# Plain float32 output and query projections, early low parts on VectorE, and six held PSUM banks in layer 1's expert matrix product

## The chip, the cores and the metric

The kernel runs on one core of one Trainium2 chip. The metric is the device time of one execution in microseconds: the median of 3 runs is 4076.9 us (4074.23 to 4081.48). The engines are named as the profile names them: PE (TensorE's matrix multiply; PEld is its weight load), DVE (VectorE), ACT (ScalarE), POOL (GpSimd), SP (the engine that issues most loads). Each runs its own instructions strictly in the order in which they stand in its queue; a semaphore wait at the head holds back all that is behind it.

## The reference

Two layers over 512 latent tokens and 256 context tokens of width 1024. Layer 0 mixes tokens with a state-space model, layer 1 with latent attention. Each is followed by an output projection, a residual and a layer norm, and by a PEER channel mixer with 16,384 experts:

```python
h = layer_norm(ALPHA * h + mod[2] * (y @ w_o))              # after the mixer
t = h * (1 + mod[4]) + mod[3]
q = (t @ w_q).reshape(n_tok, 8, 2, 64)                      # queries, 8 heads
s = einsum('thsd,hsnd->thsn', q, keys); sv, si = top_k(s, 16)
# top 16 of the 16 x 16 sums per head -> 128 experts idx and gates per token
act = gelu(einsum('td,tkd->tk', t, u_tab[idx])) * gate
f = einsum('tk,tkd->td', act, v_tab[idx])
h = layer_norm(ALPHA * h + mod[5] * f)
```

All is float32, and the choice of experts (top_k) hangs on small differences of the scores.

## The kernel before

Tokens stand in six tiles of 128: tiles 0 and 1 are the context, 2 to 5 the latents. In layer 0 the PEER mixer treats tiles 2 to 5 as *dense* and 0, 1 as *gathered*; in layer 1 tiles 4, 2, 3 are dense, 5 is gathered, and the context needs no output. A gathered tile fetches its 256 rows of `peer_u` and `peer_v` per token position by indirect DMAs on POOL's queue (`gather`, L1275), and DVE multiplies each (L1282, L1287). Dense tiles are multiplied with all experts: a block is 128 experts, `dense_u` (L1137) forms Gelu(U·H) for one block and all dense tiles, DVE multiplies it with the gates, and L1207 multiplies the result `A` with the block's rows of V. The gates come from `gate_matrix`: one-hot matrices `e` and `o` on DVE and ACT, products `g_ps` on PE (L1102), written to memory as `gm` and read back as `Gt`.

TensorE reads float32 in two ways here. A plain float32 matmul stands twice in the trace. An F32R matmul runs once, at lower precision; to keep the precision the kernel splits both operands into a high and a low part and adds three products (high·high, high·low, low·high). `split` (L302 to L306) makes the parts: ACT casts the high part (L305), and DVE or POOL, as the caller says, subtracts it (L306).

Order of the work: `merge` interleaves Python generators by clocks that the program keeps (the numbers that the generators yield), `pipeline(steps, n)` issues the preparation of a step n steps ahead of its work, and the tile framework then places the instructions on each engine. After the mixer of a layer, `out_steps` (output projection of a pair of tiles, 16 steps of 128 input rows by 512 output columns, then the norms) and `query_steps` (transpose, then 8 heads of the query projection) of the pairs run beside `route` (the top-16 searches, almost all DVE) of the tiles whose queries are ready, and beside `ahead`, which does the U products of some blocks early and stores them in memory (`ged`): blocks 0 to 39 in layer 0 and 0 to 47 in layer 1. Then come the gate matrices with the rest of these early blocks, and then `dense` beside `gather`. `dense` accumulates 8 blocks in PSUM for one half of the 1024 columns at a time and then adds the banks into `oacc` in SBUF (L1213, L1215); the U products of 8 blocks stand between; the last half group is done tile by tile (L1228). All PSUM tiles share 8 banks of 128x512 float32. SBUF tiles come from shared rings (`t4`: 20 of 4 KB, `t2`: 8 of 2 KB, `row`: 5 of 4 KB), so a load waits until an earlier tile of its place is no longer read.

Stages of the profiled execution, by their landmarks: to 374 us the state-space layer; 374 to 675 output and query projections of layer 0 with the routing of the context; 675 to 1130 routing of the latents, early blocks and gate matrices; 1130 to 2354 `dense` of layer 0; 2354 to 2668 attention; 2668 to 2790 projections of layer 1; 2790 to 3155 routing, early blocks and gate matrices; 3155 to 4040 `dense` of layer 1; then the last norms.

Of the kernel before, what the change touches and what calls it, by code (L numbers as in the profile page):

```python
# [41 lines left out]
NPOOL = 0  # L42
FA = 1.0
R0, R1 = 2.25, 3.0
A0, A1 = 40, 48
GA = 3
TL, PW, XM = 3, 2, 2.0
FG0, FG1 = 50.0, 5.0
# [59 lines left out]
class Net:  # L108
# [662 lines left out]
    def out_steps(self, l, pair, src, parts, first, rows):  # L771


        nc = self.nc
        st = {}

        def begin(_):
            st["y"] = parts()
            return 0.0

        def prep(hf, k):
            if (hf, k) == (1, 0):
                st["h"] = []
                for ti in pair:
                    h = self.t4([128, D], "h")
                    self.load(h, first(ti))
                    st["h"].append(h)
            w = self.t2([128, 512], "wo")
            self.load(w, src[k * 128:(k + 1) * 128, hf * 512:(hf + 1) * 512])
            W = self.t4([128, 2, 512], "Wos", F32R)  # L790
            self.split(W[:, 0], W[:, 1], w, nc.gpsimd if k % 4 else nc.vector)
            return W

        def work(hf, k, W):
            if k == 0:
                st["op"] = [self.ps([128, 512], "op") for _ in pair]
            for i, op in enumerate(st["op"]):
                for n, (x, y) in enumerate(((0, 0), (0, 1), (1, 0))):
                    nc.tensor.matmul(out=op, lhsT=st["y"][k // 2][:, x, k % 2, i * 128:(i + 1) * 128], rhs=W[:, y],
                                     start=(k == 0 and n == 0), stop=(k == KD - 1 and n == 2))  # L800
# [17 lines left out]
        return ([(lambda: None, begin)]  # L818
                + [(lambda hf=hf, k=k: prep(hf, k), lambda W, hf=hf, k=k: work(hf, k, W)) for hf in range(2) for k in range(KD)]
                + [(lambda: None, norm)])  # L820

    def s5_layer(self, dense, gather):
# [23 lines left out]
                    self.row_bc(a["ln_b"], 0, "lnb", tile=tile)]  # L846

        def out(pair):
            s = 1 if pair[0] < 2 else 0
            per = (2, 4)[s]  # L850
            r0 = pair[0] * 128 - (256, 0)[s]

            def parts():
                ys = []
                for x in range(4):
                    ys.append(self.t4([128, 2, 2, 256], "ys", F32R))
                    y = self.yT[s][2 * x // per][:, 2 * x % per:2 * x % per + 2, r0:r0 + 256]
                    self.split(ys[-1][:, 0], ys[-1][:, 1], y, nc.gpsimd)
                return ys

            return self.out_steps(0, pair, a["s5_w_o"], parts,
                                  lambda ti: a["ctx"][0, ti * 128:(ti + 1) * 128, :] if ti < 2
                                  else a["x"][0, (ti - 2) * 128:(ti - 1) * 128, :], lambda: self.rows2)

# [9 lines left out]
        def memory_ctx(_):  # L874
            self.rows2 = rows(1, self.big)
            return 0.0

        Hc = self.t16([128, 2, KD, 256], "Hc", F32R)
        self.h1 = {}
        (m0, q0), (m1, q1), (m2, q2) = (self.query_steps(0, (0, 1), lambda: Hc),  # L880
                                        self.query_steps(0, (2, 3), lambda: self.Hall[:, :, :, 0:256]),
                                        self.query_steps(0, (4, 5), lambda: self.Hall[:, :, :, 256:512]))
# [25 lines left out]
    def query_steps(self, l, pair, H):  # L908
# [5 lines left out]
        st = {}  # L914

        def modulate(i, ti):
            mT = self.mod_transpose(self.h1[pair][i], l, s, 3)
            c = slice(i * 128, (i + 1) * 128)
            H_ = H()
            self.split(H_[:, 0, :, c], H_[:, 1, :, c], mT, nc.vector)  # L920
            if ti not in self.tiles:
                m = self.m[ti] = self.t4([128, D], "m")
                for k4 in range(2):
                    tp = self.ps([128, 4, 128], "m_ps")
                    for k in range(4):
                        PE.transpose(out=tp[:, k, :], in_=mT[:, k4 * 4 + k, :], identity=self.ident)
                    S.copy(out=m[:, k4 * 512:(k4 + 1) * 512], in_=tp)
            return 1.0

        def prep(h):  # L930
            w = self.row([128, KD, 128], "wq")
            self.load(w, self.a["peer_w_q"][l, h])
            W = [self.t4([128, KD, 128], f"wq{x}", F32R) for x in range(2)]
            self.split(W[0], W[1], w, nc.gpsimd)
            return W

        def work(h, W):
            if h == 0:
                st["q"] = [self.t4([128, 8, 128], "qT") for _ in pair]
            if h % 2 == 0:  # L940
                st["p"] = self.ps([128, 2, 256], "qp")
            n = 0
            for k in range(KD):
                for x, y in ((0, 0), (0, 1), (1, 0)):
                    PE.matmul(out=st["p"][:, h % 2], lhsT=W[x][:, k, :], rhs=H()[:, y, k, :], start=(n == 0),
                              stop=(n == 3 * KD - 1))
                    n += 1
# [357 lines left out]
    def peer_out(self, l, ti, f, rows=None):  # L1305
# [5 lines left out]
        V.tensor_tensor(out=f, in0=f, in1=m5, op=ALU.mult)  # L1311
# [18 lines left out]

    def dense_out(self, l, ti):
        f = self.oacc[self.tiles.index(ti)]
        self.dump(f"f{l}_{ti}", f)
        return self.peer_out(l, ti, f, self.rows)


    def mla(self, dense, gather):
# [179 lines left out]
        order = gather + dense  # L1517

        def out(pair):
            q0 = (min(pair) - 2) * 128  # L1520

            def parts():
                os = []
                for o in oT:
                    os.append(self.t4([128, 2, 2, 256], "os", F32R))
                    for i, ti in enumerate(pair):
                        c = slice(i * 128, i * 128 + 128)
                        self.split(os[-1][:, 0, :, c], os[-1][:, 1, :, c], o[:, :, (ti - 2) * 128:(ti - 1) * 128], V)
                return os

            return self.out_steps(1, pair, a["mla_w_o"], parts, lambda ti: self.hd[ti], lambda: r)
# [8 lines left out]
        self.aheads = self.ahead(1, A1, 4)  # L1540
# [82 lines left out]
```

## Time and profile before

| | |
|---|---|
| median of 3 runs | 4076.9 us (4074.23 to 4081.48) |
| profiled execution | 4075.69 us; its span, first to last instruction, 4073.6 us |
| PE busy | 3664.2 us, 90% of the span |
| PEld busy | 3029.0 us, 74% |
| DVE busy | 3231.9 us, 79% |
| ACT busy | 1558.1 us, 38% |
| POOL busy | 1638.1 us, 40% |
| granted PE clock, mean | 0.953 of full speed |

Busy times are unions over an engine's instructions. A matmul's row is longer than the distance to the next, since matmuls overlap; what a matmul costs in a row of many is the distance between two starts. "Idle before" is the time in which the engine stood still just ahead of the instructions of a group, with what ended it.

### The profile page before, as it was taken

To read this page: it belongs to the slowest core of one execution; us is meant where nothing else is said; L and a number is where in the kernel's file an instruction comes from. 1 tells how busy PE (TensorE), PEld (TensorE's weight loads), DVE (VectorE), ACT (ScalarE), POOL (GpSimd) and SP (SyncE) were. 2 spreads that over 40 slices of the span, in tenths; PEclk is the share of its full clock that TensorE was granted. 3 is DMA by queue.
4 is the path that set the end of the run, shared out by engine and by line. 5 is a ranking of instruction groups with operands and counts; after the bars stand their busy time and mean duration, and the time that the engine had idled before them with its cause. 6 is when DMAs were issued, how large, how long until landed. Compare 5 with 4: busy or idle time off the path is not lost.

```text
span 4073.6 us, 54069 instructions
## 1 busy us (share of the span) xinstructions
PE 3664.2 (90%) x18795; PEld 3029.0 (74%) x18795; DVE 3231.9 (79%) x6315; ACT 1558.1 (38%) x2804; POOL 1638.1 (40%) x1140
## 2 busy tenths in 40 slices
PE   5759879789789999999999989989888899999998
PEld 3527868678667888778888855568888678999997
DVE  8784498988877788988888844469987678888887
ACT  1321335357632322233332233354467333433333
POOL 4744346245412455556555300055344113334341
PEclk6879989899999999999999999999899999999999
DMA  5457234268988899999999820044377888887885
GB/s 178 136 175 249 86 122 156 90 220 272 326 302 293 300 341 342 332 352 340 338 336 342 324 103 3 30 160 149 126 232 256 316 277 321 295 336 283 335 294 215
DMA packets 398450, 986.15 MB, mean 242 GB/s; under 512 B 67040, under 2 KB 147424, under 8 KB 393568
## 3 DMA queue, kind: packets, MB, share of 16 engines
q1 hardware_dynamic: 217120, 501.34, 35.3%
q0 software_dynamic: 110592, 402.70, 28.0%
q10 hardware_dynamic: 70464, 78.65, 5.6%
q8 instruction: 148, 2.42, 0.2%
q14 instruction: 126, 1.03, 0.1%
HBM read 892.28 MB, written 90.21 MB: 241 GB/s over the span
## 4 chain that ended last, share of the span: by engine, by line
PE 45%; issue 10%; DVE 10%; DMA 5%; POOL 5%; ACT 3%; ACTq 0%; POOLq 0%; DVEq 0%; SPq 0%
PE s_ps L1137 20%; PE acc L1207 15%; POOL row L1275 4%; PE g_ps L1102 3%; DMA row<-in_peer_v,idx 2%; DMA W<-in_peer_v 1%; DVE row L1282 1%; PE op_mla L1507 1%; DMA ge<-ged 1%; DVE e L1080 1%; DVE Ws L306 1%; PE acc L1228 1%; DVE f L1287 1%; PE kvp L1365 1%; ACT o L1085 1%
## 5 line engine op out<-in xcount | busy, mean ns | idle before, releaser
L1207 PE MATMUL acc<-Ws,A 128*128 128x512 f32 x5208 | 1202.9, 392 | 63.6 <-ACT A L305 36.3
L1137 PE MATMUL s_ps<-Hs,Uh 128*128 128x512 f32 (+1 forms) x4096 | 1184.8, 371 | 11.2 <-ACT Uh L305 11.2
L1207 PEld LDWEIGHTS acc<-Ws,A 128*128 128x128 f32 x5208 | 981.8, 189 | 280.4 <-ACT A L305 37.0
L1137 PEld LDWEIGHTS s_ps<-Hs,Uh 128*128 128x128 f32 x4096 | 761.5, 190 | 104.9 <-ACT Uh L305 12.6
L1275 POOL DMA_INDIRECT row<-in_peer_u,idx x384 | 513.2, 1336 | 783.2 <-DVE row L1282 712.3
L1137 PE MATMUL s_ps<-Hs,Ul 128*128 128x512 f32 (+1 forms) x2048 | 756.9, 370 | 15.5 <-POOL Ul L306 15.5
L1275 POOL DMA_INDIRECT row<-in_peer_v,idx x384 | 485.6, 1264 | 549.0 <-DVE f L1287 484.8
L1282 DVE SCALAR_TENSOR_TENSOR row<-row,m 128x1024 f32<-128x1024 f32 x384 | 490.4, 1293 | 54.7 <-DMA row<-in_peer_u,idx 53.8
L1287 DVE SCALAR_TENSOR_TENSOR f<-row,act,f 128x1024 f32<-128x1024 f32 x381 | 487.3, 1279 | 39.4 <-DMA row<-in_peer_v,idx 38.4
L305 ACT CAST Ws<-W 128x512 fp32r<-128x512 f32 x512 | 305.5, 619 | 489.0 <-DMA W<-in_peer_v 439.5
L1137 PEld LDWEIGHTS s_ps<-Hs,Ul 128*128 128x128 f32 x2048 | 389.0, 190 | 66.2 <-POOL Ul L306 19.8
L306 DVE TENSOR_TENSOR Ws<-W,Ws 128x512 fp32r<-128x512 f32 x512 | 345.1, 684 | 101.6 <-ACT Ws L305 101.0
L305 ACT CAST Uh<-U 128x1024 fp32r<-128x1024 f32 x256 | 268.1, 1048 | 313.6 <-DMA U<-in_peer_uT 242.6
L306 POOL TENSOR_TENSOR Ul<-U,Uh 128x1024 fp32r<-128x1024 f32 x88 | 227.3, 2585 | 312.3 <-ACT Uh L305 199.0
L1140 ACT ACTIVATE ge<-s_ps 128x512 f32<-128x512 f32 (+1 forms) x256 | 139.1, 544 | 520.4 <-PE s_ps L1137 504.9
L1102 PE MATMUL g_ps<-o,o 128*128 128x128 f32 x1792 | 232.7, 289 | 87.2 <-DVE o L1088 51.7
L1102 PEld LDWEIGHTS g_ps<-o,o 128*128 128x128 f32 x1792 | 223.7, 202 | 96.9 <-ACT o L1085 95.1
L306 POOL TENSOR_TENSOR Wos<-wo,Wos 128x512 fp32r<-128x512 f32 x60 | 87.0, 1476 | 469.9 <-PE tp_ps L286 350.9
L305 ACT CAST A<-ge 128x512 fp32r<-128x512 f32 (+1 forms) x256 | 144.5, 565 | 280.7 <-DVE ge L1188 266.6
L306 DVE TENSOR_TENSOR Ul<-U,Uh 128x1024 fp32r<-128x1024 f32 x168 | 204.9, 1221 | 47.9 <-ACT Uh L305 47.5
L1188 DVE TENSOR_TENSOR ge<-ge,Gt 128x512 f32<-128x512 f32 (+1 forms) x256 | 155.7, 619 | 74.8 <-ACT ge L1140 51.1
L306 DVE TENSOR_TENSOR A<-ge,A 128x512 fp32r<-128x512 f32 (+1 forms) x256 | 158.4, 620 | 45.6 <-ACT A L305 44.7
(346 smaller groups left out, 4631.7 us busy)
## 6 DMA issues: line engine op xcount, KB each, us to landing
U<-in_peer_uT SPq DMA_DIRECT2D x256, 512.0 KB
W<-in_peer_v SPq DMA_DIRECT2D x512, 256.0 KB
gm<-stage ACTq DMA_DIRECT2D x28, 2048.0 KB
ada_wt<-in_ada_w SPq DMA_DIRECT2D x96, 512.0 KB
Gt<-gm SPq DMA_DIRECT2D x16, 2048.0 KB
Gt<-gm SPq DMA_DIRECT2D x16, 1536.0 KB
wq<-in_peer_w_q SPq DMA_DIRECT2D x40, 512.0 KB
wo<-in_s_w_o SPq DMA_DIRECT2D x48, 256.0 KB
```

Of the source, the lines that this page charges most:

```text
L305: self.nc.scalar.copy(out=hi, in_=x)
L306: lo_eng.tensor_tensor(out=lo, in0=x, in1=hi.bitcast(F32), op=ALU.subtract)
L1080: V.tensor_tensor(out=e.rearrange("p s t (i x) -> p (s t) i x", x=2), in0=self.iota128.rearrange("p (i x) -> p i x", x=2).unsqueeze(1).to_ ...
L1085: S.copy(out=o2, in_=e[:, 0])
L1102: PE.matmul(out=gp[:, t, :], lhsT=o[1][:, t4 * 4 + t, :], rhs=o[0][:, t4 * 4 + t, :], start=True, stop=True)
L1137: PE.matmul(out=sp, lhsT=x[:, k, :], rhs=self.Hs[:, y, k, :], start=(n == 0), stop=(n == 3 * KD - 1))
L1140: S.activation(out=ge, in_=sp, func=AF.Gelu)
L1188: V.tensor_tensor(out=gv, in0=gv, in1=Gt[b // SB][:, :, :, b % SB, :], op=ALU.mult)
L1207: PE.matmul(out=acc[hf][d], lhsT=A[b][:, x, c], rhs=Ws[:, y], start=(j == 0 and n == 0), stop=(j == SB - 1 and n == 2))
L1275: GP.indirect_dma_start(out=r, out_offset=None, in_=tab, in_offset=bass.IndirectOffsetOnAxis(ap=ik[:, k:k + 1], axis=0), element_offset=l ...
L1282: x = V.scalar_tensor_tensor(out=r, in0=r, scalar=1.0, in1=m, op0=ALU.mult, op1=ALU.mult, accum_out=act[:, k:k + 1])
L1287: x = V.scalar_tensor_tensor(out=f, in0=r, scalar=act[:, k:k + 1], in1=f, op0=ALU.mult, op1=ALU.add)
```

## The change

Four edits. (1) `out_steps` takes the weights `wo` and the activations as they are: one plain float32 product per step and tile instead of three F32R products, and no split of either operand. (2) `query_steps` does the same with `wq` and the transposed tile; the split of the activations stays where the dense tiles need it for `dense_u`. (3) `ahead` lets DVE instead of POOL make the low part of U, and takes a list of blocks; in layer 1 these are the first 3 of each 8 blocks (48 as before). (4) Layer 1 uses a new `dense_held`: six PSUM banks (three tiles by two halves) collect all 128 blocks, U and V products alternate block by block, the V rows are loaded and split 1024 wide, and the last KL = 2 blocks are multiplied tile by tile; `peer_out` then reads the banks. Layer 0 keeps `dense`.

```diff
-A0, A1 = 40, 48
+A0, A1 = 40, 3
+KU, LH, KL, GQ = 2, 4, 2, 4
 # out_steps
             w = self.t2([128, 512], "wo")
             self.load(w, src[k * 128:(k + 1) * 128, hf * 512:(hf + 1) * 512])
-            W = self.t4([128, 2, 512], "Wos", F32R)
-            self.split(W[:, 0], W[:, 1], w, nc.gpsimd if k % 4 else nc.vector)
-            return W
+            return w
...
-                for n, (x, y) in enumerate(((0, 0), (0, 1), (1, 0))):
-                    nc.tensor.matmul(out=op, lhsT=st["y"][k // 2][:, x, k % 2, i * 128:(i + 1) * 128], rhs=W[:, y], ...)
+                nc.tensor.matmul(out=op, lhsT=y(i, k), rhs=W, start=(k == 0), stop=(k == KD - 1))
 # query_steps
-            W = [self.t4([128, KD, 128], f"wq{x}", F32R) for x in range(2)]
-            self.split(W[0], W[1], w, nc.gpsimd)
-            return W
+            return w
...
-                for x, y in ((0, 0), (0, 1), (1, 0)):
-                    PE.matmul(out=st["p"][:, h % 2], lhsT=W[x][:, k, :], rhs=H()[:, y, k, :], ...)
+            for i in range(2):
+                for k in range(KD):
+                    PE.matmul(out=st["p"][:, h % 2, i * 128:(i + 1) * 128], lhsT=W[:, k, :], rhs=st[i][:, k, :], ...)
 # ahead
-        yield from pipeline([(lambda b=b: self.dense_u_prep(l, b, self.nc.gpsimd), lambda Us, b=b: work(b, Us))
-                             for b in range(n)], LA)
+        yield from pipeline([(lambda b=b: self.dense_u_prep(l, b, self.nc.vector), lambda Us, i=i: work(i, Us))
+                             for i, b in enumerate(blocks)], LA)
+    def dense_held(self, l):
...
+        def products(b, d, Ws):
+            c = slice(d * 128, (d + 1) * 128)
+            for n, (x, y) in enumerate(((0, 0), (0, 1), (1, 0))):
+                for hf in range(2):
+                    PE.matmul(out=acc[d][hf], lhsT=A[b][:, x, c], rhs=Ws[y][:, hf * 512:(hf + 1) * 512],
+                              start=(b == 0 and n == 0), stop=(b == NB - 1 and n == 2))
...
+        steps = us[:KU]
+        for b in range(NB):
+            steps += us[b + KU:b + KU + 1] + [vs[b]]
+        steps += [(lambda: None, lambda _, d=d: finish(d)) for d in range(NT)]
+        yield from pipeline(steps, LH)
 # peer_out
+            for hf in range(2):
+                c = slice(hf * 512, (hf + 1) * 512)
+                V.tensor_tensor(out=f[:, c], in0=acc[hf], in1=m5[:, c], op=ALU.mult)
 # peer
-        merge(self.dense(l), self.gathering)
+        merge(self.dense_held(l) if len(self.tiles) < 4 else self.dense(l), self.gathering)
```

Three places in the queues. First, DVE in layer 0 while it routes a context tile (the rows with `rw` are top-16 searches); the low part of the output weights stands among them:

```order
L976 MAX_INDEX rw_4008<-rw_4008,tk_tmp 128x8
L975 MAX rw_4008<-tk_tmp 128x8
L306 TENSOR_TENSOR Wos<-wo,Wos 128x512
L976 MAX_INDEX rw_4008<-rw_4008,tk_tmp 128x8
L972 MAX rw_4008<-scr 128x8
```

and the same engine there now, where only the evictions `res` of the finished products are left among the searches:

```order
L950 MAX_INDEX rw_3987<-rw_3987,tk_tmp 128x8
L948 MATCH_REPLACE tk_tmp<-rw_3987,cand 128x80
L797 TENSOR_TENSOR res<-op,m_3937 128x512
L949 MAX rw_3987<-tk_tmp 128x8
L797 TENSOR_TENSOR res<-op,m_3937 128x512
```

The split of the weights is gone from the searches. Second, POOL before, at the end of layer 0's queries, where the low parts of the early blocks follow the indirect loads of the gather:

```order
L306 TENSOR_TENSOR wq_5358<-wq,wq_5357 128x1024
L1275 DMA row<-in_peer_u,idx 128x1024
L306 TENSOR_TENSOR Ul<-U,Uh 128x1024 x22
L1275 DMA row<-in_peer_u,idx 128x1024
L306 TENSOR_TENSOR Ul<-U,Uh 128x1024
```

and DVE now, in the routing of the first latent tile, where they stand between the searches:

```order
L946 MAX rw_4789<-cand 128x8
L949 MAX rw_4789<-tk_tmp 128x8
L947 MAX_INDEX rw_4789<-rw_4789,cand 128x8
L306 TENSOR_TENSOR Ul<-U,Uh 128x1024
L950 MAX_INDEX rw_4789<-rw_4789,tk_tmp 128x8
```

POOL keeps indirect loads alone. Third, PE at the start of layer 1's expert product before, where the V products of all 48 early blocks follow in one run:

```order
L1137 MATMUL s_ps<-Hs,Uh 128x384 x2
L1137 MATMUL s_ps<-Hs,Ul 128x384
L1207 MATMUL acc_25631<-Ws,A 128x512 x3
L1207 MATMUL acc_25632<-Ws,A 128x512 x3
L1207 MATMUL acc_25633<-Ws,A 128x512 x3
```

and now, where the last tile's products of the first block are followed by a block of U products:

```order
L1180 MATMUL acc_24481<-Wh,A 128x512
L1180 MATMUL acc_24482<-Wh,A 128x512
L1180 MATMUL acc_24481<-Wl,A 128x512
L1180 MATMUL acc_24482<-Wl,A 128x512
L1180 MATMUL acc_24481<-Wh,A 128x512
L1180 MATMUL acc_24482<-Wh,A 128x512
L1111 MATMUL s_ps<-Hs,Uh 128x384 x2
```

PE now alternates between two banks of one tile, and V and U blocks alternate.

## Rows read from the trace of the kernel before

**Rows 1.** Windows: us, each engine's busy us, then PE clock, DMA share, GB/s.

```profile
374.00:675.00 301.00, 250.76 (x1756) 226.18 (x1755) 196.65 (x699) 117.21 (x208) 131.31 (x76) 0.93 0.41 137
675.00:1130.00 455.00, 371.40 (x2137) 319.20 (x2136) 396.77 (x1026) 252.83 (x442) 199.87 (x105) 0.93 0.67 226
...
2668.00:2790.00 122.00, 108.72 (x671) 94.19 (x670) 91.21 (x243) 68.38 (x131) 78.59 (x41) 0.97 0.48 155
2790.00:3155.00 365.00, 311.88 (x1957) 301.43 (x1957) 317.40 (x892) 212.72 (x365) 164.79 (x79) 0.93 0.60 195
3155.00:4040.00 885.00, 861.00 (x4217) 767.13 (x4216) 709.51 (x1023) 324.19 (x551) 282.91 (x225) 0.99 0.84 305
4040.00:4074.00 34.00, 15.26 (x68) 12.30 (x66) 23.92 (x45) 4.22 (x6) 0.00 (x0) 0.76 0.18 71
```

**Rows 2.** Groups of lines: PE from 535.5 to 680, DVE from 490 to 590.

```profile
L799 PE MATMUL op<-Wos,ys 128*128 128x512 f32 x192 | 52.9, 434 | 28.3 <-DVE Wos L306 26.0 <-POOL Wos L306 1.2 <-ACT Wos L305 1.1
...
L306 DVE TENSOR_TENSOR Wos<-wo,Wos 128x512 fp32r<-128x512 f32 x5 | 4.5, 898 | 0.0
```

**Rows 3.** Timeline pieces: start, us, what, count; F32R and plain float32 matmuls.

```profile
2672.70 34.66 PE L799 MATMUL op<-Wos,os 128*128 128x512 f32 x151
...
673.51 6.69 PE L945 MATMUL qp<-Hs,wq 128*128 128x256 f32 x55
...
497.76 28.41 PE L762 MATMUL zp<-yl,wg 128*128 128x128 f32 x253
...
2491.79 0.19 PEld L1507 LDWEIGHTS op_mla<-pT,v 128*128 128x128 f32 x1 [0.24 <-issue]
...
2495.65 0.19 PEld L1507 LDWEIGHTS op_mla<-pT,v 128*128 128x128 f32 x1 [0.24 <-issue]
```

**Rows 4.** Timeline of POOL and DVE around 2800 us, and of DVE at 524 us.

```profile
2799.60 2.40 POOL L306 TENSOR_TENSOR Ul<-U,Uh 128x1024 fp32r<-128x1024 f32 x1 [0.80 <-ACT Uh L305]
...
2799.64 4.58 DVE L1041 TENSOR_TENSOR oh<-iota,ab 128x2048 bf16<-128x2048 bf16 x2
...
524.59 1.22 DVE L1041 TENSOR_TENSOR oh<-iota,ab 128x2048 bf16<-128x2048 bf16 x1
```

**Rows 5.** Groups of lines on DVE while latents are routed, layer 0, 657 to 850.

```profile
L1041 DVE TENSOR_TENSOR oh<-iota,ab 128x2048 bf16<-128x2048 bf16 x8 | 13.9, 1764 | 0.0
...
L1036 DVE TENSOR_TENSOR ab<-rw 128x128 bf16<-128x128 f32 x4 | 3.2, 798 | 0.1
```

**Rows 6.** The same in layer 1, 2764 to 2960.

```profile
L1041 DVE TENSOR_TENSOR oh<-iota,ab 128x2048 bf16<-128x2048 bf16 x6 | 13.7, 2308 | 0.0
```

**Rows 7.** Groups on DVE among the gate matrices: 850 to 1130, then 2960 to 3155.

```profile
L1282 DVE SCALAR_TENSOR_TENSOR row<-row,m 128x1024 f32<-128x1024 f32 x62 | 94.8, 1540 | 13.2 <-DMA row<-in_peer_u,idx 13.2
...
L1080 DVE TENSOR_TENSOR e<-iota,iT 128x2048 bf16<-128x2048 bf16 x39 | 60.9, 1561 | 26.1 <-ACT iT L1070 25.0 <-PE s_ps L1137 1.2
```

**Rows 8.** Costliest groups of the page: the low part of U on either engine.

```profile
L306 POOL TENSOR_TENSOR Ul<-U,Uh 128x1024 fp32r<-128x1024 f32 x88 | 227.3, 2585 | 312.3 <-ACT Uh L305 199.0 <-issue 47.1 <-DVE rw L975 28.7
...
L306 DVE TENSOR_TENSOR Ul<-U,Uh 128x1024 fp32r<-128x1024 f32 x168 | 204.9, 1221 | 47.9 <-ACT Uh L305 47.5
```

**Rows 9.** Waits (us, times, longest): 675 to 1130, then 2790 to 3155.

```profile
POOL Ul L306 <- ACT Uh L305: 78.2, 19, 15.1
...
POOL Ul L306 <- ACT Uh L305: 117.3, 32, 10.8
```

**Rows 10.** Layer 1's expert product: waits from 3150 to 3420, PE group from 3150.

```profile
PE acc L1207 <- ACT A L305: 14.3, 1, 14.3
...
L1207 PE MATMUL acc<-Ws,A 128*128 128x512 f32 x2232 | 514.3, 391 | 24.0 <-ACT A L305 14.3 <-DVE Ws L306 6.9 <-ACT Ws L305 2.8
```

**Rows 11.** Timeline of the end: PE, then the first and last of DVE.

```profile
4038.78 16.48 PE L1228 MATMUL acc<-Ws,A 128*128 128x512 f32 x72
...
4044.42 0.69 DVE L1231 TENSOR_TENSOR oacc<-acc,oacc 128x512 f32<-128x512 f32 x1 [2.95 <-PE acc L1228]
...
4068.80 1.22 DVE L268 TENSOR_TENSOR h<-h,lnb 128x1024 f32<-128x1024 f32 x1
```

More of the change, by code (lines that the diff above doesn't have):

```diff
@@ L55 @@
 AT = 2
-E0, E1, E2 = 0, 11, 5
-YB, YC = 1, 17
+E0, E1, E2 = 0, 10, 5
 NF, MV = 2, (11, 13, 15)
@@ L769, in glu, with out_steps @@
             nc.vector.tensor_tensor(out=y, in0=y, in1=sg[:, x * per:(x + 1) * per, :], op=ALU.mult)
-    def out_steps(self, l, pair, src, parts, first, rows):
+    def out_steps(self, l, pair, src, y, first, rows):
         nc = self.nc
         st = {}
-        def begin(_):
-            st["y"] = parts()
-            return 0.0
         def prep(hf, k):
@@ L816, in norm @@
             return 0.0
-        return ([(lambda: None, begin)]
-                + [(lambda hf=hf, k=k: prep(hf, k), lambda W, hf=hf, k=k: work(hf, k, W)) for hf in range(2) for k in range(KD)]
+        return ([(lambda hf=hf, k=k: prep(hf, k), lambda W, hf=hf, k=k: work(hf, k, W)) for hf in range(2) for k in range(KD)]
                 + [(lambda: None, norm)])
@@ L848, in out @@
         def out(pair):
[L849 to L861, printed above, removed]
+            return self.out_steps(0, pair, a["s5_w_o"], lambda i, k: self.y_tile(pair[i], k),
                                   lambda ti: a["ctx"][0, ti * 128:(ti + 1) * 128, :] if ti < 2
@@ L916, in modulate @@
         def modulate(i, ti):
[L917 to L921, printed above, removed]
+            mT = st[i] = self.mod_transpose(self.h1[pair][i], l, s, 3)
+            if ti in self.tiles:
+                c = slice(i * 128, (i + 1) * 128)
+                H_ = H()
+                self.split(H_[:, 0, :, c], H_[:, 1, :, c], mT, nc.vector)
+            else:
                 m = self.m[ti] = self.t4([128, D], "m")
@@ L1155, in ahead, with prep_g, prep_u, work_u @@
             yield 1.0
-        yield from pipeline([(lambda b=b: self.dense_u_prep(l, b, self.nc.gpsimd), lambda Us, b=b: work(b, Us))
-                             for b in range(n)], LA)
+        yield from pipeline([(lambda b=b: self.dense_u_prep(l, b, self.nc.vector), lambda Us, i=i: work(i, Us))
+                             for i, b in enumerate(blocks)], LA)
+    def dense_held(self, l):
+        nc, a = self.nc, self.a
+        V, S, PE = nc.vector, nc.scalar, nc.tensor
+        NT = len(self.tiles)
+        TD = NT * 128
+        NB, SB = 128, 8
+        Gt, A, last = {}, {}, {}
+        acc = self.acc = []
+        def prep_g(sb):
+            Gt[sb] = self.t16([128, NT, 4, 8, 32], "Gt")
+            self.load(Gt[sb], self.gm[sb])
+        def prep_u(b):
+            if b == 0:
+                prep_g(0)
+            if b % SB == GQ and b // SB + 1 < NB // SB:
+                prep_g(b // SB + 1)
+            if b in self.early:
+                ge = self.t2([128, TD], "ge")
+                self.load(ge, self.ged[self.early[b]])
+                return ge
+            return self.dense_u_prep(l, b, V)
+        def work_u(b, x):
+            ge = x if b in self.early else self.dense_u(x)
+            gv = ge.rearrange("p (d g t) -> p d g t", d=NT, g=4)
+            V.tensor_tensor(out=gv, in0=gv, in1=Gt[b // SB][:, :, :, b % SB, :], op=ALU.mult)
+            A[b] = self.t4([128, 2, TD], "A", F32R)
+            self.split(A[b][:, 0], A[b][:, 1], ge, V)
+            return 0.0 if b in self.early else 5.2 * NT / 4
+        def prep_v(b):
+            W = self.spare([128, D], "W")
+            self.load(W, a["peer_v"][l * NEXP + b * 128:l * NEXP + (b + 1) * 128, :])
+            Wh, Wl = self.t4([128, D], "Wh", F32R), self.t4([128, D], "Wl", F32R)
+            self.split(Wh, Wl, W, V)
+            return Wh, Wl
+        def products(b, d, Ws):
[4 more added lines that the diff above has]
+                              start=(b == 0 and n == 0), stop=(b == NB - 1 and n == 2))
+        def work_v(b, Ws):
+            if b == 0:
+                acc.extend([self.ps([128, 512], f"acc{d}") for hf in range(2)] for d in range(NT))
+            if b >= NB - KL:
+                last[b] = Ws
+                return 0.0
+            for d in range(NT):
+                products(b, d, Ws)
+            return 5.2 * NT / 4
+        def finish(d):
+            for b in last:
+                products(b, d, last[b])
+            return 1.3 * KL
+        yield from self.aheads
+        us = [(lambda b=b: prep_u(b), lambda x, b=b: work_u(b, x)) for b in range(NB)]
+        vs = [(lambda b=b: prep_v(b), lambda x, b=b: work_v(b, x)) for b in range(NB)]
+        steps = us[:KU]
[3 more added lines that the diff above has]
+        yield from pipeline(steps, LH)
@@ L1331, in dense_out @@
     def dense_out(self, l, ti):
-        f = self.oacc[self.tiles.index(ti)]
-        self.dump(f"f{l}_{ti}", f)
+        f = (self.acc if len(self.tiles) < 4 else self.oacc)[self.tiles.index(ti)]
         return self.peer_out(l, ti, f, self.rows)
@@ L1519, in out @@
         def out(pair):
[L1520 to L1531, printed above, removed]
+            return self.out_steps(1, pair, a["mla_w_o"],
+                                  lambda i, k: oT[k // 2][:, k % 2, (pair[i] - 2) * 128:(pair[i] - 1) * 128],
+                                  lambda ti: self.hd[ti], lambda: r)
         p, q = tuple(order[:2]), tuple(order[2:])
@@ L1539, in mla @@
         self.gathering = self.gather(1, R1)
-        self.aheads = self.ahead(1, A1, 4)
+        self.aheads = self.ahead(1, [b for b in range(128) if b % 8 < A1], 4)
         self.gates = self.gate_matrices(4)
```

33 lines of the change are left out of this document (16 added, 17 removed).

## The prediction

> **What bounds the kernel now.** I read the windows by stage first, then PE's groups and its idle time in the two stages of projections, the pitch of each kind of matmul in the timeline, DVE's and POOL's groups where the low parts move, and last the waits and the end. The reader is to see three kinds of stage in [rows 1]. In layer 1's expert product (3155 to 4040) PE is busy 861.0 of 885 us: there only PE's idle time can be won. In the routing and gate stages DVE is the fullest engine (396.8 of 455 us and 317.4 of 365), so what is added to DVE there is paid and what is taken off is won. In the projections neither is full: PE is busy 250.8 of 301 us in layer 0, and stands 28.3 us ahead of the output products, 26.0 of it waiting for five low parts of weights, `Wos`, that DVE makes in 0.898 us each but only when they get through its row of searches [rows 2].
>
> The sum is made against the profiled execution, 4075.69 us; the median is 1.2 us above it, which I add at the end.
>
> **A. Plain products, layer 0.** F32R matmuls of 512 columns start 0.2285 us apart: (34.66 − 0.39)/150, the last one's own time taken off; of 256 columns 0.1187: (6.69 − 0.28)/54. A plain one of 128 columns stands twice, (28.41 − 0.275)/252 = 0.1117 a record, and of 512 columns (2495.65 − 2491.79)/9 = 0.429 a record [rows 3]. The last two come from other lines with the same shapes. A pair's output goes from 96 × 0.2285 = 21.9 to 64 × 0.429 = 27.5 us (+5.5), its queries from 192 × 0.1187 = 22.8 to 256 × 0.1117 = 28.6 (+5.8). Three pairs of layer 0 add 34 us to PE. The last queries (5.8) lie beside routing, where DVE is the bound. PE has 301 − 250.8 = 50.2 us idle in this stage; apart from the 28.3 of `Wos` that is 22, and I let half of it, 11, take up work: 34 − 5.8 − 11 = +17. Against it, the `Wos` idle goes (−28.3), and with it the slowness of the products behind each pause: 192 of them were busy 52.9 us [rows 2] where their pitch gives 43.9 (−9; the granted clock in the stage is 0.93 [rows 1]). A = 17 − 28.3 − 9 = −20. Next late there is DVE with the context's routing; it loses the five `Wos` and the context's splits, and its searches wait for queries, which come sooner. Bounds: −37 if all idle takes up work, 0 if DVE sets the end (a rival below).
>
> **B. Low parts on DVE, routing of the latents, layer 0.** On POOL a low part took 2.585 us, 88 times; on DVE 1.221, 168 times [rows 8]. So 88 × 1.221 = 107 us come to DVE, in the stages where it is the bound. What comes back stands in [rows 4]: while POOL's `Ul` ran, the same `oh` took 2.29 us a piece, and 1.22 without it. In the 193 us of [rows 5], `oh` lost 8 × (1.764 − 1.22) = 4.4 and `ab` 4 × (0.798 − 0.28) = 2.1 us; over about nine such groups of two-input operations I come to 25. About 23 low parts fall into that stretch: 28 to be paid. B = +3 (bounds −25 if they only fill idle, +28 if nothing comes back).
>
> The Trainium skill, "SBUF — State Buffer", section "Who interferes with whom", says that VectorE and GpSimd share one port pair under an exclusive lock, and that nothing else between them contends; 2.29 against 1.22 us in [rows 4] agrees. By that rule the give-back ends where POOL has no arithmetic left, so the indirect loads that POOL keeps would take nothing from DVE; no row here shows it.
>
> **C. Gate matrices.** Between 850 and 1130 the gather's products lost 62 × (1.540 − 1.22) = 19.8 us, with `e` and `o` about 32; 17 low parts cost 20.7. Between 2960 and 3155 `e` lost 39 × (1.561 − 1.22) = 13.3, with the other groups about 32; 21 low parts cost 25.6 [rows 7]. So DVE's load falls by 12 and 7 us. DVE is not full here (it waits 13.2 us for rows and 26.1 for ACT), so I put −5 on the path; bounds −19 and 0.
>
> **D. Projections of layer 1.** Products before: 2 × 21.9 + 2 × 22.8 = 89.5 us by pitch in a window of 122, with 95 other matmuls; so some 20 us are idle or off pitch (13.3 are idle [rows 1]). The change adds 2 × 5.5 + 5.8 up to the first routing, 16.8, and takes away the splits of weights and activations ahead of the products. These about cancel: D = −1, bounds −4 and +17.
>
> **E. Routing, layer 1.** In [rows 6] `oh` lost 6 × (2.308 − 1.22) = 6.5, all groups about 22; 27 low parts cost 33. +11, of which DVE's idle time there takes a little: E = +8, bounds −12 and +33.
>
> **F. Held banks.** PE's work is the same: 128 blocks × 18 products (2232 and 72 before [rows 10, 11]) and 80 blocks of U. From 3155 to PE's last end, 4038.78 + 16.48 = 4055.3, are 900.3 us with 861.0 + 15.3 busy: 24.0 idle. 14.3 of this is one wait for the first `A` [rows 10], which needs the first gates from memory and stays. The other 10 come from weights whose splits on DVE or ACT are late; with U and V blocks alternating, DVE's need per block is even, and 96 additions into `oacc` of 0.69 us [rows 11] go, 66 us of a DVE that is busy 709.5 of 885 us. F = −10, bounds −24 (all idle goes) and +16 (a rival below).
>
> **G. The end.** DVE works through three tiles from 4044.42 to 4070.02, 8.5 us each, and the span ends 18.3 us after PE [rows 11]. Now a tile's last two blocks are 12 products, 2.7 us, so the first tile is ready 5.5 us before PE's end T. Without the addition into `oacc` I take 8 us a tile: DVE is done at T − 5.5 + 24 = T + 18.5, and with the 3.6 us from DVE's last to the span's end (4073.6 − 4070.0) the span ends at T + 22. G = +4, bounds 0 and +8.
>
> Sum: −20 + 3 − 5 − 1 + 8 − 10 + 4 = −21, that is 4055 in the profiled execution and 4056 at the median.
>
> **Rivals.**
>
> *R1, slower: DVE inherits POOL's wait.* A `Ul` needs `Uh`, ACT's cast, and ACT's queue has Gelu ahead of it, which needs PE. POOL stood 78.2 and 117.3 us for it [rows 9] with only the gather behind it; now searches and one-hot matrices stand behind it. If DVE takes over a quarter of these 195.5 us, 49, the sum is −21 + 49 = +28: 4105. It decides from a mean stall of (21 + 8)/88 = 0.33 us per `Ul`. For it: DVE itself waited 47.5 us for `Uh` over its 168 [rows 8], 0.28 each. Against: POOL's waits are those of an engine that had nothing else to do, while DVE has 193/23 = 8 us of other work between two low parts, in which `Uh` is cast.
>
> *R2, no change: PE's idle in A was not the bound.* If DVE's searches of the context set when latent routing starts, A is 0, the rest −1: 4076. For it: DVE is at 197 of 301 us and nearly full late in the stage. Against: its searches wait for PE's queries, too.
>
> *R3, more: the port pays twice.* If C is wholly on the path (−19 in place of −5) and E is taken up by idle (0 in place of +8): −21 − 14 − 8 = −43, 4033. For it: the gather behind POOL's low parts runs sooner, too, and ends C's 13.2 us wait for rows. Against: ACT and PE set part of those stages.
>
> *R4, the held banks don't do what they should.* Six of eight banks are held, and two remain for U products and their Gelu. If each of the 80 U blocks makes PE wait 0.2 us for a bank, F is +16 in place of −10: +5, 4082. For it: PE starts the next block only when ACT has read the bank before. Against: a V block of 18 products, 4.1 us, stands between two U blocks.
>
> *R5, slower: DVE pays its low parts in full.* If the losses in [rows 5, 6] come from something other than POOL's `Ul`, B is +28 and E +33: −21 + 25 + 25 = +29, 4106. For it: both stages have DVE as the fullest engine. Against: [rows 4] has the same instruction at both durations within one routing pattern. The Trainium skill, "Perfetto Trace Analysis", section "Optimizing Scalar/DVE Operations", points this way: it advises moving work off a saturated VectorE, and doubts only that a move between engines that share a port helps.
>
> **How the numbers follow.** What a measurement of this kernel can tell from no change is about 0.2%, 8 us. Forecast 0.45 (of it 0.44 faster, 0.01 same), R3 0.22, R2 0.12 (0.10 same, 0.01 on each side), R4 0.08 (half same, half slower), R1 0.11, R5 0.02. Faster: 0.44 + 0.22 + 0.01 = 0.67; same: 0.01 + 0.10 + 0.04 = 0.15; slower: 0.01 + 0.04 + 0.11 + 0.02 = 0.18. The range reaches from 4022 (R3 with F near its lower bound) to 4090 (R4 with E at 16); the forecast's own is 4038 to 4070, from A between −28 and −10 and E between 0 and 16.
>
> **What would show it.** Right: no `Wos` and no idle of PE on DVE ahead of `op`, though its records are 0.43 apart; queries at 0.112 a record; `oh` at a mean near 1.22; latent routing starting some 20 us sooner; PE's idle in layer 1's expert product near 14 us at its start; PE's end to the end of the span about 22. Wrong: DVE standing ahead of `Ul` for over 0.3 us each, mainly for ACT's `Uh` (R1); PE standing for a bank at `s_ps` (R4); plain 512-column records longer than 0.43 us, each 0.05 of which costs five pairs 16 us; DVE without idle before latent routing, with PE done long before (R2).

## The result and the profile after

The changed kernel takes 4108.2 us (median of 4 runs, 4104.54 to 4108.89) against 4076.4 for the kernel before: a ratio of 1.0068, 95% interval 1.0048 to 1.0088 (the medians alone give 1.0078). It is slower by some 30 us where 20 us faster was forecast, and above the range's upper end of 4090. Its profiled execution has a span of 4105.9 us against 4073.6.

To see where these 32.3 us went I cut both spans at the same landmarks: the end of the last query product of layer 0, of the last `rw` of its searches, of its last `g_ps`, and so on. The last four columns belong to experiments below (plain products alone, low parts on GpSimd, low parts a step later, and the best version). All numbers are us of one profiled execution each.

| stage | before | after | plain | GpSimd | later | best |
|---|---|---|---|---|---|---|
| to the last query product, layer 0 | 680.3 | 666.5 | 664.5 | 664.7 | 662.7 | 664.6 |
| searches of the latents | 151.5 | 150.6 | 143.5 | 143.7 | 153.0 | 148.1 |
| gate matrices, layer 0 | 264.3 | **291.7** | 265.2 | 265.2 | 259.2 | 257.0 |
| expert product 0, attention, projections 1 | 1692.0 | 1697.2 | 1696.4 | 1693.4 | 1689.8 | 1690.1 |
| searches, layer 1 | 172.4 | 175.5 | 169.4 | 169.2 | 170.6 | 162.0 |
| gate matrices, layer 1 | 192.1 | **201.0** | 191.3 | 191.2 | 179.6 | 178.9 |
| expert product 1, to PE's end | 902.7 | 904.5 | 904.7 | 906.1 | 902.1 | 903.0 |
| from PE's end to the span's end | 18.3 | 18.9 | 18.3 | 19.0 | 19.0 | 19.2 |

The loss is in the gate matrices: +27.4 and +8.9. Windows of these two stages in the changed kernel (columns as in [rows 1]):

```profile
818.00:1109.00 291.00, 229.88 (x1421) 204.14 (x1420) 218.30 (x265) 191.26 (x350) 82.81 (x54) 0.94 0.77 252
...
2981.00:3183.00 202.00, 165.03 (x1102) 162.24 (x1103) 146.61 (x173) 135.54 (x247) 36.74 (x27) 0.94 0.74 243
```

and in the kernel before:

```profile
832.00:1096.00 264.00, 223.18 (x1410) 198.98 (x1409) 231.70 (x247) 189.88 (x351) 133.19 (x73) 0.95 0.82 275
...
2960.00:3153.00 193.00, 164.51 (x1104) 161.53 (x1103) 157.77 (x155) 135.58 (x249) 95.86 (x47) 0.94 0.76 251
```

DVE is busy 13.4 and 11.2 us *less* although 18 and 20 low parts were added, and yet the stages are longer: DVE's idle time, window less busy, goes from 32.3 to 72.7 and from 35.2 to 55.4 us. These 40.4 and 20.2 us more, less the 24.6 us of load that fell away, make the loss of the two stages. DVE's groups in the first of the two, changed kernel:

```profile
L1054 DVE TENSOR_TENSOR e<-iota,iT 128x2048 bf16<-128x2048 bf16 x60 | 73.1, 1219 | 0.7 <-ACT iT L1044 0.7
L1330 DVE SCALAR_TENSOR_TENSOR row<-row,m 128x1024 f32<-128x1024 f32 x56 | 67.6, 1218 | 0.0
...
L306 DVE TENSOR_TENSOR Ul<-U,Uh 128x1024 fp32r<-128x1024 f32 x18 | 22.1, 1225 | 65.6 <-ACT Uh L305 65.6
```

`e` and `row` are at 1.22 us, where `row` had 1.540 here and `e` 1.561 in layer 1 [rows 7]: the time that they lost beside POOL's `Ul` did come back. But DVE waits 65.6 us ahead of 18 low parts for ACT's cast `Uh`, 3.6 us each. The main waits of that stage in the changed kernel (us in total, times, longest):

```profile
PEld g_ps L1076 <- ACT o L1059: 68.5, 36, 7.4
PE g_ps L1076 <- ACT o L1059: 44.0, 30, 6.3
DVE Ul L306 <- ACT Uh L305: 65.6, 18, 9.0
ACT ge L1114 <- PE s_ps L1111: 38.5, 13, 5.0
ACT o L1059 <- DVE e L1054: 37.3, 22, 4.0
```

in layer 1's gate stage, changed kernel:

```profile
DVE Ul L306 <- ACT Uh L305: 51.6, 19, 4.3
```

and in layer 0's gate stage of the kernel before, where POOL waits for the cast:

```profile
PE g_ps L1102 <- ACT o L1085: 24.8, 24, 2.2
...
ACT o L1085 <- DVE e L1080: 23.6, 15, 10.2
...
POOL Ul L306 <- ACT Uh L305: 14.2, 5, 4.5
```

The waits close a ring: DVE for ACT, ACT for PE and DVE, PE for ACT. One turn of it in the timeline of the changed kernel (start, us):

```profile
917.62 0.96 DVE L1062 TENSOR_TENSOR o<-e,gT 128x768 f32<-128x768 bf16 x1
...
918.50 1.22 DVE L1330 SCALAR_TENSOR_TENSOR row<-row,m 128x1024 f32<-128x1024 f32 x1
...
920.80 3.73 PE L1076 MATMUL g_ps<-o,o 128*128 128x128 f32 x32
921.00 0.60 ACT L1114 ACTIVATE ge<-s_ps 128x512 f32<-128x512 f32 x1 [2.19 <-PE s_ps L1111]
...
922.37 1.05 ACT L1059 CAST o<-e 128x1024 f32<-128x1024 bf16 x1
...
923.92 1.54 ACT L1078 COPY stage<-g_ps 128x512 f32<-128x512 f32 x3
925.33 1.08 ACT L305 CAST Uh<-U 128x1024 fp32r<-128x1024 f32 x1
926.44 1.23 DVE L306 TENSOR_TENSOR Ul<-U,Uh 128x1024 fp32r<-128x1024 f32 x1 [6.72 <-ACT Uh L305]
927.59 1.22 DVE L1054 TENSOR_TENSOR e<-iota,iT 128x2048 bf16<-128x2048 bf16 x1
```

ACT stands at Gelu until PE has finished a block of U (921.00), then works off an `o`, copies and only then the cast (925.33). DVE has stood at `Ul` for 6.72 us by then; the next `e`, whose one-hots PE needs for the next `g_ps`, starts at 927.59.

The other parts in the changed kernel. PE in layer 0's output and queries (groups), then the pitch in layer 1 (timeline):

```profile
L920 PE MATMUL qp<-mT,wq 128*128 128x128 f32 x512 | 58.0, 275 | 0.0
L791 PE MATMUL op<-wo,yl 128*128 128x512 f32 x128 | 57.5, 609 | 5.3 <-DMA wo<-in_s_w_o 5.3
```

```profile
2711.80 19.48 PE L791 MATMUL op<-wo,oT 128*128 128x512 f32 x45
...
2744.39 5.86 PE L920 MATMUL qp<-mT,wq 128*128 128x128 f32 x51
```

PE waits 5.3 us there, for a load, where it stood 28.3 [rows 2]; the pitches are (19.48 − 0.592)/44 = 0.429 and (5.86 − 0.275)/50 = 0.112, as worked out from [rows 3]. DVE in the searches of layer 0, changed kernel (643 to 817), where `oh` had 1.764 [rows 5]:

```profile
L306 DVE TENSOR_TENSOR Ul<-U,Uh 128x1024 fp32r<-128x1024 f32 x21 | 25.3, 1210 | 0.1
...
L1015 DVE TENSOR_TENSOR oh<-iota,ab 128x2048 bf16<-128x2048 bf16 x7 | 8.3, 1216 | 0.0
```

PE in layer 1's expert product, changed kernel, where [rows 10] had 24.0 us idle before the `acc` products:

```profile
L1180 PE MATMUL acc<-Wh,A 128*128 128x512 f32 x1536 | 426.6, 391 | 12.2 <-ACT A L305 12.2
L1111 PE MATMUL s_ps<-Hs,Uh 128*128 128x384 f32 x1326 | 341.8, 339 | 4.3 <-ACT Uh L305 4.3
...
L1111 PE MATMUL s_ps<-Hs,Ul 128*128 128x384 f32 x664 | 225.2, 339 | 6.6 <-DVE Ul L306 6.6
```

The idle time left the `acc` products but for the first wait, and came up before the U products, 10.9 us.

### The profile page after: what moved, and what is told of

It reads as the page before. It is cut to its first block, busy times and chain, and to the rows that moved or that the text cites. A ratio compares the mean times of both kernels' runs of the same rounds, so it can differ in the third digit from the quotient of the medians.

```text
span 4105.9 us, 52738 instructions
## 1 busy us (share of the span) xinstructions
PE 3719.0 (91%) x18955; PEld 3031.4 (74%) x18955; DVE 3068.7 (75%) x6143; ACT 1450.2 (35%) x2527; POOL 1238.6 (30%) x940
## 3 DMA queue, kind: packets, MB, share of 16 engines
q0 software_dynamic: 110592, 402.70, 27.4%
## 4 chain that ended last, share of the span: by engine, by line
PE 57%; DVE 14%; issue 12%; DMA 7%; POOL 6%; ACT 3%; SPq 0%; POOLq 0%; ACTq 0%; DVEq 0%
PE s_ps L1111 20%; PE acc L1180 8%; PE acc L1255 8%; POOL row L1323 5%; PE qp L920 3%; PE op L791 3%; DMA U<-in_peer_uT 3%; DMA row<-in_peer_v,idx 2%; PE g_ps L1076 2%; PE zp L762 2%; DVE Ul L306 1%; PE op_mla L1560 1%; DVE w L645 1%; PE yp L697 1%; DMA row<-in_peer_u,idx 1%
## 5 line engine op out<-in xcount | busy, mean ns | idle before, releaser
L1255 PE MATMUL acc<-Ws,A 128*128 128x512 f32 x2976 | 689.1, 393 | 37.5 <-ACT A L305 21.4
L1255 PEld LDWEIGHTS acc<-Ws,A 128*128 128x128 f32 x2976 | 564.3, 190 | 160.6 <-ACT A L305 21.9
L1323 POOL DMA_INDIRECT row<-in_peer_v,idx x384 | 502.9, 1310 | 516.8 <-DVE f L1335 460.7
L306 DVE TENSOR_TENSOR Ul<-U,Uh 128x1024 fp32r<-128x1024 f32 x256 | 312.0, 1219 | 281.8 <-ACT Uh L305 273.6
L1330 DVE SCALAR_TENSOR_TENSOR row<-row,m 128x1024 f32<-128x1024 f32 x384 | 461.0, 1218 | 42.7 <-DMA row<-in_peer_u,idx 41.7
L1180 PE MATMUL acc<-Wh,A 128*128 128x512 f32 x1536 | 426.6, 391 | 12.2 <-ACT A L305 12.2
L1180 PEld LDWEIGHTS acc<-Wh,A 128*128 128x128 f32 x1536 | 288.3, 188 | 66.7 <-ACT A L305 12.6
L305 ACT CAST Ws<-W 128x512 fp32r<-128x512 f32 x256 | 152.1, 619 | 264.3 <-DMA W<-in_peer_v 217.7
L1180 PE MATMUL acc<-Wl,A 128*128 128x512 f32 x768 | 237.5, 390 | 0.0
L306 DVE TENSOR_TENSOR Ws<-W,Ws 128x512 fp32r<-128x512 f32 x256 | 174.3, 684 | 56.0 <-ACT Ws L305 55.7
```

Source lines behind the costliest of these rows:

```text
L305: self.nc.scalar.copy(out=hi, in_=x)
L306: lo_eng.tensor_tensor(out=lo, in0=x, in1=hi.bitcast(F32), op=ALU.subtract)
L1180: PE.matmul(out=acc[d][hf], lhsT=A[b][:, x, c], rhs=Ws[y][:, hf * 512:(hf + 1) * 512], start=(b == 0 and n == 0), stop=(b == NB - 1 and n ...
L1255: PE.matmul(out=acc[hf][d], lhsT=A[b][:, x, c], rhs=Ws[:, y], start=(j == 0 and n == 0), stop=(j == SB - 1 and n == 2))
L1323: GP.indirect_dma_start(out=r, out_offset=None, in_=tab, in_offset=bass.IndirectOffsetOnAxis(ap=ik[:, k:k + 1], axis=0), element_offset=l ...
L1330: x = V.scalar_tensor_tensor(out=r, in0=r, scalar=1.0, in1=m, op0=ALU.mult, op1=ALU.mult, accum_out=act[:, k:k + 1])
```

## The experiments

Two theories stand against each other. Theory W: edit 3 costs time because its subtractions close the ring of waits. Theory L: it costs time by the load that they bring to VectorE. Code cuts are shortened. Ratios are to the kernel before, run beside each kernel on the same chip, with 95% intervals; times of different groups are not compared.

**Low parts back on GpSimd** (changed kernel, undoing edit 3's choice of engine):

```diff
-self.dense_u_prep(l, b, self.nc.vector)
+self.dense_u_prep(l, b, self.nc.gpsimd)
```

> The changed kernel with the early low parts back on GpSimd (the list of blocks, the plain products and the held banks stay). Stage by stage the changed kernel stands to the kernel before as follows: the end of layer 0's queries 14 us earlier, layer 0's gate matrices 27 us longer (from the end of the searches to the last g_ps), the projections of layer 1 6.5 us longer, its routing 3 and its gate matrices 9 us longer, the expert product of layer 1 2 us longer. Theory W: the 27 and the 9 come from VectorE standing in its row at Ul for ScalarE's cast Uh, which stands behind Gelu, which waits for TensorE, which waits for the one-hots behind Ul: a ring. Theory L: they come from the added load, 88 x 1.22 us, on VectorE, and nothing is given back. Both expect the low parts on GpSimd to give back some 36 us: 4065 to 4078. If edit 3 is not the cause (the plain products or the banks are), 4100 to 4110.

The ratio is 0.9939 (0.9925 to 0.9954), 4055.0 us. That is better than expected: the gate stages are back at 265.2 and 191.2, and the searches are also 7 and 6 us shorter than with VectorE. The loss comes from edit 3's choice of engine; the rest of the change gains 0.6%.

**The subtraction a step later** (changed kernel; cast of block j, then subtraction of block j − 1, then products of block j − 2):

```diff
+for j in range(n + LA):
+    if j < n:        # load U; nc.scalar.copy(out=Uh, in_=U)
+    if 0 < j <= n:   # nc.vector.tensor_tensor(out=Ul, U - Uh) of block j - 1
+    if j >= LA:      yield work(j - LA, lo.pop(j - LA))
```

> The changed kernel, with VectorE's subtraction for an early block issued one early block later than ScalarE's cast of that block (same instructions, same engines, same load). Theory W: VectorE's waits for Uh, 65.6 us in layer 0's gate stage and 51.6 in layer 1's, fall below 20 us each, the gate stages lose most of the 27 and 9 us, time 4072 to 4090. Theory L: VectorE has the same 107 us of low parts to do, so 4104 to 4112, with idle time of VectorE only renamed.

The ratio is 0.9907 (0.9892 to 0.9923), 4044.2 us. DVE's waits of layer 0's gate stage, this kernel:

```profile
DVE Ul L1143 <- ACT Uh L1138: 16.9, 5, 6.8
DVE e L1054 <- ACT iT L1044: 15.4, 3, 8.5
```

and 19.9 us for `Uh` in layer 1's. Engines and load are the same, so W holds and L falls. I missed the size: the stages lost 32.5 and 21.4 us and are now 5 and 12.5 *below* the kernel before.

**The cast on VectorE too, in the gates** (changed kernel):

```diff
+if len(self.routed) + len(self.gat) == n_tiles: nc.vector.tensor_copy(out=Uh, in_=U)
+else: nc.scalar.copy(out=Uh, in_=U)
```

> The changed kernel, with the cast Uh of the 38 early blocks that are issued once all tiles are routed moved from ScalarE to VectorE, right ahead of the subtraction. This is more load for VectorE (38 casts of an estimated 0.6 to 1.2 us, by Ul's 1.22 as the nearest, 23 to 46 us), but nothing on VectorE waits for ScalarE's row any more. Theory W: gate stages shorter in spite of the load, 4080 to 4098. Theory L: longer by the load, 4125 to 4155.

The ratio is 0.9957 (0.9942 to 0.9972), 4061.7 us, below even the range of W. Two groups of DVE in layer 0's gate stage, this kernel:

```profile
L1140 DVE TENSOR_TENSOR Ul<-U,Uh 128x1024 fp32r<-128x1024 f32 x18 | 22.1, 1226 | 3.0 <-ACT Uh L1139 1.4
L1137 DVE CAST Uh<-U 128x1024 fp32r<-128x1024 f32 x17 | 11.7, 689 | 10.9 <-DMA U<-in_peer_uT 10.9
```

With more load on DVE, and 1.4 us of wait for ACT ahead of `Ul` instead of 65.6, the stage takes 263 us against 291.7. Added load has shortened it, which rules L out a second time.

**One block more ahead** (changed kernel, cast and subtraction still back to back): `LA, LD = 2, 5` becomes `3, 5`.

> The changed kernel with the early blocks prepared three steps ahead in place of two, VectorE's subtraction still directly behind ScalarE's cast. Theory W (VectorE stands because cast and subtraction are issued back to back, and ScalarE's row stands at Gelu): more distance to TensorE's use does not part the two, so VectorE's wait for Uh in layer 0's gate stage stays over 45 us (65.6 in the changed kernel) and the ratio at 1.003 to 1.008. Rival S (the blocks are only prepared too late for TensorE): as good as parting the two, 0.990 to 0.995.

The ratio is 1.0078 (1.0065 to 1.0091). DVE's wait in layer 0's gate stage, this kernel:

```profile
DVE Ul L306 <- ACT Uh L305: 67.1, 17, 9.2
```

One block more of lead changes neither the wait nor the time, as W expects, so rival S falls.

**Blocks by halves in layer 1** (changed kernel): `self.dense_held(l)` becomes `self.dense(l)`, early blocks `range(48)`.

> The changed kernel with layer 1 on the product by halves of the kernel before (early blocks 0 to 47, additions into oacc, last half group tile by tile). From the end of layer 1's gate matrices to TensorE's end the changed kernel takes 904.5 us and the kernel before 902.7, and the ends differ by 0.6: held banks give nothing, so 4100 to 4110. If the held banks gained their 10 us and something else in the stage took them, 4112 to 4122.

The ratio is 1.0077 (1.0062 to 1.0093), 4113.2 us. This decides nothing: the time lies in the second range, but the kernel before took 4083.6 us on that chip, and the ratio times the 4076.4 us of the first comparison gives 4107.8, in the first range. The interval overlaps that of the changed kernel.

**Plain products alone** (low parts on GpSimd and blocks by halves together: edits 1 and 2 are left).

> The kernel before with edits 1 and 2 alone (plain products for output and queries in both layers; early low parts on GpSimd, blocks by halves in layer 1). With the low parts on GpSimd the changed kernel was 0.61% under the kernel before. Theory P: nearly all of that is edits 1 and 2, by my terms A and D, since the held banks give next to nothing: ratio 0.993 to 0.996. Theory H: the held banks carry a good part of it and the half-wise product looked as good only because the ring hid it: ratio 0.996 to 1.000.

The ratio is 0.9930 (0.9917 to 0.9943), 4055.1 us: P holds. By the table the queries of layer 0 end 15.8 us sooner and the searches are 8.0 and 3.0 us shorter.

**Split products in layer 1** (the version a step later, with layer 1's output and queries as in the kernel before):

> The kernel with the subtraction a step later (0.9907 of before), with layer 1's output and queries back on three F32R products and splits (layer 0 stays plain). From the first output product to the last query product of layer 1 the kernel before took 296.8 us and the one with the subtraction a step later 302.5. If term D's size was off because TensorE is full there, 5 to 6 us come back: ratio 0.989 to 0.990. If the splits cost as much as they save by then, 0.9902 to 0.9915.

The ratio is 0.9915 (0.9902 to 0.9927), the second case. From the first output product `op` to the last query product layer 1 took 118.1 us in place of 119.6, the searches behind them 175.5 in place of 170.6. (The 296.8 and 302.5 us of the expectation begin at `op_mla`, a product of the attention, some 181 us ahead of the first output product.)

**GpSimd in the searches, VectorE a step later in the gates:**

```diff
+done = len(self.routed) + len(self.gat) == n_tiles
+(nc.vector if done else nc.gpsimd).tensor_tensor(out=Ul, in0=U, in1=Uh, op=ALU.subtract)
```

> The kernel with the subtraction a step later, the subtractions on GpSimd while tiles are still searched and on VectorE once all are routed. With GpSimd the stage of the latents' searches took 143.9 us in layer 0 against 153.2 with VectorE a step later, and 169.2 against 170.6 in layer 1; the gate stages are shorter with VectorE a step later (259.2 against 265.2 and 179.6 against 191.2). If the two stages are independent, 9 to 10 us under the version with a step later: ratio 0.988 to 0.989. If VectorE's losses beside GpSimd (my rows 5 and 6) eat what its load gives back, 0.990 to 0.992.

The ratio is 0.9850 (0.9838 to 0.9863), 4022.3 us, the best version: 58 us under the kernel before on that chip, and more than expected.

**Variations of the best version.** By halves in layer 1, then `LH` 4 to 6, then `LA` 2 to 3, then GpSimd's subtraction directly behind the cast:

> The best version so far (subtractions on GpSimd during the searches, on VectorE a step later in the gates; 0.985 of before) with layer 1's blocks by halves in place of the held banks. Plain products alone (by halves, low parts on GpSimd) had 0.993, with held banks 0.9939. Theory N (held banks give nothing): 0.984 to 0.9865. Theory H (held banks give my 10 us once the ring is gone): 0.9870 to 0.9885.

> The best version so far, with the loads and splits of the held product issued six steps ahead in place of four. In its expert product of layer 1 TensorE stands 12.0 us within blocks of U and 5.2 us ahead of them, and ScalarE's casts wait 245 us for U's loads. If these pauses come from U arriving late, 8 to 15 us less: 0.981 to 0.983. If the loads are limited by the rings of tiles or by memory, nothing: 0.984 to 0.986.

> The best version so far, with early blocks prepared three steps ahead in place of two, the subtraction one step behind its cast. With the two parted, VectorE still waits 16.9 and 19.9 us for Uh in the gate stages, and TensorE for the one-hots. If what is left of the wait comes from the lead, 2 to 8 us less: 0.983 to 0.9845. If the ring is gone already, no change: 0.9845 to 0.986.

> The best version so far, with GpSimd's subtractions during the searches directly behind the cast, and VectorE's in the gates a step later as before. The searches of layer 0 took 143.9 us with GpSimd at once and 148.3 a step later; of layer 1 169.2 and 162.0. If the distance matters only where an engine with other work in its row waits (VectorE), there is nothing to choose: 0.984 to 0.987.

By halves the ratio is 0.9874 (0.9859 to 0.9890): the value lies in H's range, the interval reaches into N's. Six steps of lead give 0.9965 (0.9952 to 0.9979), *worse*, which neither case had: layer 1's expert product takes 937.0 us, 903.0 in the best version. PE in this stage, with six steps and then in the best version:

```profile
L1194 PE MATMUL acc<-Wh,A 128*128 128x512 f32 x1536 | 442.1, 401 | 40.8 <-ACT A L305 40.0
L1111 PE MATMUL s_ps<-Hs,Uh 128*128 128x384 f32 x1326 | 341.1, 339 | 0.0
...
L1194 PE MATMUL acc<-Wh,A 128*128 128x512 f32 x1536 | 427.1, 391 | 9.4 <-ACT A L305 9.4
```

The idle time ahead of the U products is gone as wanted, but PE now waits 40.0 us for ACT's cast of `A`, 9.4 in the best version; what makes ACT late there was not tried. Three steps of lead and GpSimd at once give 0.9886 (0.9870 to 0.9901) and 0.9893 (0.9877 to 0.9908): no gain, and both lie above everything that was expected. By stages each trades one for another: three steps shorten layer 1's searches (152.9 us against 162.0) and lengthen the gates (262.7 and 183.3 against 257.0 and 178.9); GpSimd at once shortens layer 0's searches (143.7 against 148.1) and lengthens layer 1's (169.3 against 162.0).

**Held banks against halves on one chip**, both kernels once more:

> The best version (held banks) once more, beside the version by halves on the same chip. By its first comparison 0.985; if the chips differ in this ratio by what the version by halves suggests, 0.985 to 0.988.

> The version by halves once more. Theory N (held banks give nothing, as the stage's 903.0 against 903.4 us says): within 0.0015 of the held version's ratio. Theory H (held banks give 10 us): 0.0020 to 0.0035 above it.

The ratios are 0.9864 (0.9848 to 0.9880) and 0.9873 (0.9856 to 0.9890): 0.0009 apart, within the bound of theory N. Held banks give nothing that can be told, but a gain of a few us is not excluded: each interval is 0.003 wide, and the expert product took 898.5 us here against 901.5 by halves, 903.0 against 903.4 in the two kernels' first runs.

## Why the prediction was wrong

By stage, forecast and measured in us:

| term | forecast | measured | |
|---|---|---|---|
| A plain products, layer 0 | −20 | −13.8 | right, somewhat large |
| B searches, layer 0 | +3 | −0.9 | near, but see below |
| C gate matrices | −5 | **+36.3** | wrong, outside its bounds of −19 and 0 |
| D up to layer 1's last query | −1 | +5.2 | off, inside the bounds; +3.6 in the projections |
| E searches, layer 1 | +8 | +3.1 | near, but see below |
| F held banks | −10 | +1.8 | wrong |
| G the end | +4 | +0.6 | inside the bounds |

**C is the step that failed.** Its arithmetic was right: "DVE's load falls by 12 and 7 us", and it fell by 13.4 and 11.2. What failed is "bounds −19 and 0": they priced a load and left out the wait that the same instructions bring. R1 had that mechanism, but I gave it 0.11, by an argument from the searches alone: "DVE has 193/23 = 8 us of other work between two low parts, in which `Uh` is cast". This holds in the searches: DVE waits 0.1 us ahead of 21 low parts in layer 0, 7.3 ahead of 27 in layer 1. In the gates it does not hold: there ACT has Gelu, one-hots and copies ahead of the cast and waits for PE and DVE itself. [rows 9] gave half a hint: of POOL's 117.3 us 53.6 lay in layer 1's gates (2960 to 3153), but of its 78.2 only 14.2 in layer 0's. That R1's time, 4105, is almost the measured one is luck: it put 49 us of wait on the path, while DVE stood 117.2 us for `Uh` in the gates alone, part of it in place of other idle time. With cast and subtraction a step apart C is (259.2 − 264.3) + (179.6 − 192.1) = −17.6, near the lower bound that the load alone gives.

**A** kept its mechanism. From 535.6 (540.6 now) the output products end after 64.4 us in place of 84.5, and the queries take 61.7 in place of 60.4. The pauses went as forecast; I left out that PE would wait 5.3 us for the weights' loads, and the 5.0 us that these products start later. That R2 was no case is shown by the queries' end, 13.8 us sooner.

**B and E** are near by luck, for each hides a second effect. Against the kernel before they are −0.9 and +3.1. Against the changed kernel with low parts on GpSimd, which prices the low parts alone, they are 150.6 − 143.7 = +6.9 and +6.3, 13 in all where I had 11: the give-back of [rows 4 to 6] was sized well, and R5 falls. That searches became 8.0 and 3.0 us shorter by plain products alone was in no term. The traces show where it comes from: when layer 0's last query product ends, DVE has done 24 search rounds over `cand` with plain products alone and 16 before, being busy 158.1 us since 374 instead of 202.0; so 24 rounds are left instead of 32. In layer 1, too, 24 are left instead of 30.

**D**: in all kernels with plain products in layer 1 the way from its first output product to its last query product takes 119.6 us, in the kernel before 116.0: of the 16.8 us added, 3.6 stay. I let all of it be taken up. The other 1.6 us lie ahead of the projections, and two profiled executions of one kernel differ by more in this stage (by halves, 1694.7 and 1697.2 us). Split products give back 1.5 of the 3.6 and lose 4.9 in the searches behind, so plain ones can stay.

**F**: the wait for the first `A` stayed, as forecast (12.2 us), and "the other 10" went, but as many came up ahead of the U products. What makes `Uh` and `Ul` late there stays open: ACT stood 219.0 us for V's loads and 65.2 for U's in this stage before, and stands 259.8 us for U's alone now. R4's wait for banks is not in the rows: the pauses wait for `Uh` and `Ul`.

**G**: DVE starts on the first tile 5.7 us before PE's end, as forecast (5.5), but takes 7.0 us a tile where I put 8.

## What to carry to other kernels

Moving an instruction to another engine moves its wait into that engine's row. Price the wait at the place in the row, with all that stands behind it, and look for a ring: if the new engine waits for one that in turn waits for what is queued behind, the load alone does not tell the cost. Here issuing producer and consumer a step apart was the cure. More lead was no substitute for it: one block more left the ratio at 1.0078. In another product two steps more made the stage 34 us longer.

## What the runs showed of the hardware

VectorE's cast of 128x1024 float32 to F32R took 0.689 us, ScalarE's 1.05. While GpSimd issued only indirect loads, VectorE's two-input operations stayed at 1.22 us (`row` 1.218, `e` 1.219 in layer 0's gate stage of the changed kernel). Of the 99 `e` in both gate stages 52 ran while such a load was being issued, and took 1.217 to 1.225 us: here these loads took nothing from them. That is the point that the prediction left open; the trace of the kernel before has it, too, with 46 `e` beside such loads alone at 1.211 to 1.222 us.
